# Last output tile's second token half in two quarters, each with its own statistics, transposes, scaling and store

## The chip, the cores and the metric

The kernel runs on one core of a Trainium2 chip. Its metric is the device time of one execution in microseconds (us), the median of several runs. A profile is one further execution, recorded by the hardware profiler. The engines of a core are TensorE (PE: matmuls, with weight loads as PEld), VectorE (DVE), ScalarE (ACT), GpSimd (POOL) and SyncE (SP, which here issues DMAs). Each has its own instruction queue and runs it in order; semaphores tie the queues together.

## The reference

One layer of a decoder on 512 tokens of width 2048, in float32. A conditioning vector gives six vectors of modulation (shift, scale and gate, twice). A first block mixes tokens in two ways and projects back; a second is an MLP with a hidden width of 8192 and a squared ReLU; a norm closes it:

```python
x = x + gate1 * merged
h = rmsnorm(x) * (1 + scale2) + shift2
x = x + gate2 * (relu(h @ w1) ** 2 @ w2)
out = x * rsqrt(mean(x * x, axis=-1) + 1e-6) * g_final
```

## The kernel before, in words

Activations are held transposed: a tile `x1[d]` of 128 x 512 has 128 of the 2048 features in its partitions and the 512 tokens in its columns, and there are sixteen. A float32 product is made of three matmuls in the fp32r type: weights and activations are split in a high and a low part (`wh`, `wl`; the activations carry both), and high-high, high-low and low-high are summed in PSUM (lines 174 to 176, and 894 to 896 for a part of the columns). The conditioning comes first, then the projections, attention and the gated merge with matmuls of 512 columns. Most of the MLP runs as "product units" (lines 1120 to 1123), whose matmuls have 256 columns. What they leave of the second weight matrix is a last pass over a part of the hidden width, tile by tile.

That pass ends in `fin_last`. Feature tiles 0 to 13 are finished before it. It takes tiles 14 and 15 in halves of 256 tokens. `tile` multiplies a half (twelve matmuls, from `hs` tiles as the moving operand), adds the product times the gate to `x1` (VectorE), squares the sum (ScalarE) and multiplies it by the final gain (VectorE). `post` works on a half's two rows of 128 tokens, numbered r = 0 to 3. `fin_stats` sums the squares over the features with matmuls of one column into a PSUM bank (`msf`): the sum of the earlier tiles in `sq_box["f"]`, then the squares of tile 14, then of tile 15. It takes the root on ScalarE and its reciprocal on VectorE, into a small tile `rf`. `to_rows` transposes the feature tiles with TensorE into PSUM (`nt`) and copies them (line 988 on VectorE, line 990 on ScalarE) into `nat` tiles, which have tokens in their partitions and 1024 features in their columns (z = 0 or 1). `fin_out` scales each `nat` tile by `rf` in two pieces of 512 columns, one on VectorE and one on ScalarE, and sends each piece to the output with a DMA that SyncE issues (line 1018).

In the product units the work stands on the engines in the order of the code (`manual_schedule`, lines 1275 to 1366). In the tail behind them a scheduler places instructions by their dependences when the program is built; the lines below give the pieces there, not their final order. Tiles live in pools in on-chip memory. `pw` holds the streamed weights (`wr`), the split weights (`wh`, `wl`, whose matrix in the product units begins 16 elements into the tile, `shift=16` at line 1160) and the small tiles (`small`), among them `rf`. The pools `sb` (most activation tiles, by `k4`: `h`, `mh`, `t`, `ya`, `yb`, `nat`, `sq`), `xw` and `win` (`hw`) lie behind it. `hs` is allocated from the other end.

Of the kernel before, what the change touches and what calls it, by code (L numbers as in the profile page):

```python
# [13 lines left out]
AF = mybir.ActivationFunctionType  # L14
# [4 lines left out]
D = 2048  # L19
# [8 lines left out]
SF = 8  # L28
# [16 lines left out]
def _body(tc, x, c, w_ada, b_ada, g_mix, w_in, b_in, g_v, b_v, w_s, b_s, w_oa, w_ob, w_out,  # L45
# [5 lines left out]
    pe, act, dve, pool = nc.tensor, nc.scalar, nc.vector, nc.gpsimd  # L51

    with tc.tile_pool(name="const", bufs=1) as cp, \
# [6 lines left out]
        def nm(s):  # L60
            cnt[0] += 1
            return f"{s}_{cnt[0]}"
# [17 lines left out]
        def k4(shape, s, dt=F32):  # L80
            return pools["sb"][1].tile(shape, dt, name=nm(s), tag="k4", bufs=k4_bufs[0])
# [13 lines left out]
        def bank(s):  # L95
            return pp.tile([128, T], F32, name=nm(s), tag="mm", bufs=6)

        def misc(s):
            return pp.tile([128, T], F32, name=nm(s), tag="ms", bufs=2)

        def small(shape, s, bufs=2):
            return pw.tile(shape, F32, name=nm(s), tag=f"sm{shape[1]}", bufs=bufs)
# [83 lines left out]
        epsc = cp.tile([128, 1], F32, name="epsc")  # L186
# [671 lines left out]
        x1 = {}  # L858
# [8 lines left out]
        sq_box = {}  # L867
# [22 lines left out]
        HALF = [slice(0, 256), slice(256, 512)]  # L890

        def mm3h(ps, wh, wl, a, start, stop, hs):
            kw = dict(skip_group_check=True)
            pe.matmul(ps, lhsT=wh, rhs=a[:, 0, hs], start=start, stop=False, **kw)
            pe.matmul(ps, lhsT=wh, rhs=a[:, 1, hs], start=False, stop=False, **kw)
            pe.matmul(ps, lhsT=wl, rhs=a[:, 0, hs], start=False, stop=stop, **kw)
# [66 lines left out]
        hid = {}  # L963
# [13 lines left out]
        def to_rows(d, rs):  # L977
            if d == 0:
                for r in range(NR):
                    for z in range(2):  # L980
                        nat[r, z] = k4([128, 1024], "nat")
            p = misc("nt")
            for r in rs:
                pe.transpose(p[:, r * 128:(r + 1) * 128], x1[d][:, r * 128:(r + 1) * 128], ident)
            for r in rs:
                o = nat[r, d // 8][:, (d % 8) * 128:(d % 8 + 1) * 128]
                if r % 2:
                    dve.tensor_copy(o, p[:, r * 128:(r + 1) * 128])
                else:
                    act.activation(o, p[:, r * 128:(r + 1) * 128], AF.Copy)  # L990

        wfin = {}

        def fin_stats(hf, sq):
            p = bank("msf")
            for z in range(3):
                for i in range(2):
                    r = hf * 2 + i
                    t = sq[z - 1][:, i * 128:(i + 1) * 128] if z else sq_box["f"][:, r * 128:(r + 1) * 128]
                    pe.matmul(p[:, i:i + 1], lhsT=t, rhs=ones[:, 0:1], start=z == 0 and i == 0, stop=z == 2,  # L1000
                              skip_group_check=True)
            rf = small([128, 2], "rf", 2)
            act.activation(rf, p[:, 0:2], AF.Sqrt, bias=epsc, scale=1.0 / D)
            dve.reciprocal(rf, rf)
            return rf

        def fin_out(hf, rf):
            ov = out.rearrange("(r i) d -> i r d", r=NR)
            for z in range(2):
                for i in range(2):  # L1010
                    r = hf * 2 + i
                    for q in range(2):
                        t = nat[r, z][:, q * 512:(q + 1) * 512]
                        if q:
                            act.activation(t, t, AF.Copy, scale=rf[:, i:i + 1])
                        else:
                            dve.tensor_scalar(t, t, rf[:, i:i + 1], None, op0=ALU.mult)
                        nc.sync.dma_start(out=ov[:, r, z * 1024 + q * 512:z * 1024 + (q + 1) * 512], in_=t)

        def fin_last():  # L1020
            act.activation(warm, x1[13][:, 0:1], AF.Sqrt, bias=epsc, scale=0.0)
            sq = []

            def tile(d, hf):
                p = bank("w")[:, 0:256]
                h, l = wfin[d]
                for k in range(SF // 2):
                    mm3h(p, h[:, k, :], l[:, k, :], hid["t"][:, k], k == 0, k == SF // 2 - 1, HALF[hf])
                t = x1[d][:, HALF[hf]]
                dve.scalar_tensor_tensor(t, p, mod(5, d), t, op0=ALU.mult, op1=ALU.add)  # L1030
                sq.append(k4([128, 256], "sq"))
                act.activation(sq[-1], t, AF.Square)
                dve.tensor_scalar(t, t, gfin_col[:, d:d + 1], None, op0=ALU.mult)

            def post(hf):
                rf = fin_stats(hf, sq[hf * 2:])
                for d in (14, 15):
                    to_rows(d, (hf * 2, hf * 2 + 1))
                fin_out(hf, rf)

            tile(14, 0)
            tile(15, 0)
            tile(14, 1)
            post(0)
            tile(15, 1)
            post(1)

        box4 = {}

# [323 lines left out]
        def t_epi(pr, j, p):  # L1373
            d = pr * 2 + j
            dve.scalar_tensor_tensor(x1[d], p, mod(5, d), x1[d], op0=ALU.mult, op1=ALU.add)
            add_square(x1[d], d, "f")
            dve.tensor_scalar(x1[d], x1[d], gfin_col[:, d:d + 1], None, op0=ALU.mult)

        for pr in range(7):
            ws_pair(pr * 256, list(range(SF // 2, SF)), w2_p, lambda k: hid["t"][:, k - SF // 2],  # L1380
                    lambda j, p, pr=pr: t_epi(pr, j, p))
# [4 lines left out]
        def w2_keep(d):  # L1386
            def bk(h, l):
                wfin[d] = h, l
                for e in (12, 13):
                    if d == 15:  # L1390
                        to_rows(e, range(NR))
                if d == 15:
                    fin_last()
            return bk
# [23 lines left out]
```

## Time and profile before

| | us |
|---|---|
| median of 3 runs | 2648.8 (2648.76 to 2649.16) |
| profiled execution | 2651.6 |
| its span, first to last instruction | 2649.9 |
| its time outside the span | 1.7 |
| TensorE busy in the span | 2564.9 (97%) |
| VectorE busy | 1836.0 (69%) |
| ScalarE busy | 1069.6 (40%) |
| mean granted TensorE clock | 0.986 of full speed |

The sums of busy time are averages over stages with different limits. The end of the program is read from the timeline of its last 16 us, from each engine's queue and from the chain of waits; the long stages from the number of matmuls in a stretch in which TensorE never idles, which gives the time from one start to the next (a matmul's own duration in the trace is longer, as matmuls overlap).

### The profile page before, as it was taken

What the parts mean: (1) busy time and instruction counts of PE and PEld (TensorE: products, weight loads), DVE (VectorE), ACT (ScalarE), POOL (GpSimd) and SP (SyncE); (2) the same over time, 40 slices, a digit from 0 to 9 for tenths busy, and PEclk for the clock granted to TensorE, in tenths of its full rate; (3) what the DMA queues carried; (4) which work ended last, traced back from release to release, by engine and by line L of the source; (5) the groups of instructions that cost most, each with busy time, mean ns of one, the idle gap of its engine ahead of it and who ended that gap; (6) DMA issues with size and microseconds to landing.
All of it is one profiled execution on the core that took longest, in us unless ns stands there. A gap on an engine that the chain in (4) does not pass through costs nothing.

```text
span 2649.9 us, 39933 instructions
## 1 busy us (share of the span) xinstructions
PE 2564.9 (97%) x16339; PEld 2329.3 (88%) x16339; DVE 1836.0 (69%) x2392; ACT 1069.6 (40%) x1533; POOL 231.5 (9%) x254
## 2 busy tenths in 40 slices
PE   5999999999999999999999999999988999999988
PEld 4889878888888888888888999999987999999986
DVE  6894563657454453555358898989874888888876
ACT  4322232342222222232365666666663333333334
POOL 4120210000000000001100011111110000000003
PEclk8999999999999999999999999999999999999999
DMA  9973574646364564656424566666678656565642
GB/s 322 305 237 100 159 176 119 188 132 214 94 216 140 174 199 129 219 186 207 150 68 161 192 205 213 202 216 201 217 250 330 223 195 223 195 223 195 223 163 80
DMA packets 403273, 506.15 MB, mean 191 GB/s; under 512 B 14414, under 2 KB 345842, under 8 KB 398482
## 3 DMA queue, kind: packets, MB, share of 16 engines
q1 hardware_dynamic: 384304, 439.40, 52.1%
q0 software_dynamic: 18624, 64.15, 6.3%
q8 instruction: 128, 2.10, 0.3%
q14 instruction: 55, 0.45, 0.1%
q10 hardware_dynamic: 162, 0.06, 0.0%
HBM read 435.36 MB, written 68.19 MB: 190 GB/s over the span
## 4 chain that ended last, share of the span: by engine, by line
PE 65%; issue 23%; DMA 5%; POOL 3%; DVE 2%; ACT 1%; SPq 0%; POOLq 0%; ACTq 0%; DVEq 0%
PE w L176 11%; PE w L174 11%; PE w L175 11%; PE x L1120 7%; PE x L1121 7%; PE x L1123 7%; POOL hid_d L1231 2%; PE v L453 1%; PE v L454 1%; PE v L455 1%; PE q L175 1%; PE q L176 1%; PE q L174 1%; PE va L730 1%; PE va L728 1%
## 5 line engine op out<-in xcount | busy, mean ns | idle before, releaser
L142 ACT ACTIVATE wh<-wr 128x1024 fp32r<-128x1024 f32 (+2 forms) x269 | 270.4, 1007 | 796.0 <-PE w L175 535.2
L143 DVE TENSOR_TENSOR wl<-wr,wh 128x1024 fp32r<-128x1024 f32 (+2 forms) x257 | 318.7, 1241 | 368.5 <-ACT wh L142 359.3
L1120 PE MATMUL x<-hw,wh 128*128 128x256 f32 x1568 | 367.9, 277 | 11.3 <-ACT wh L142 11.3
L1121 PE MATMUL x<-hw,wh 128*128 128x256 f32 x1568 | 367.7, 277 | 0.0
L174 PE MATMUL w<-h,wh 128*128 128x512 f32 x896 | 351.8, 393 | 0.8 <-ACT wh L142 0.8
L176 PE MATMUL w<-h,wl 128*128 128x512 f32 x896 | 349.6, 390 | 0.8 <-DVE wl L143 0.8
L175 PE MATMUL w<-h,wh 128*128 128x512 f32 x896 | 349.2, 390 | 0.0
L142 ACT ACTIVATE wh<-raw 128x896 fp32r<-128x896 f32 (+1 forms) x240 | 238.8, 1000 | 177.2 <-PE x L1121 117.4
L1120 PEld LDWEIGHTS x<-hw,wh 128*128 128x128 f32 x1568 | 295.3, 188 | 11.7 <-ACT wh L142 11.7
L1121 PEld LDWEIGHTS x<-hw,wh 128*128 128x128 f32 x1568 | 295.3, 188 | 0.0
L143 DVE TENSOR_TENSOR wl<-raw,wh 128x896 fp32r<-128x896 f32 (+1 forms) x240 | 275.8, 1149 | 9.8 <-ACT wh L142 9.8
L142 ACT ACTIVATE wh<-s 128x896 fp32r<-128x896 f32 (+1 forms) x180 | 176.9, 1000 | 161.6 <-PE x L1121 160.1
L143 DVE TENSOR_TENSOR wl<-s,wh 128x896 fp32r<-128x896 f32 (+1 forms) x180 | 207.0, 1150 | 38.5 <-ACT wh L142 38.5
L1123 PE MATMUL x<-hw,wl 128*128 128x256 f32 x1568 | 214.4, 276 | 0.0
L1120 PE MATMUL x<-h,wh 128*128 128x256 f32 x896 | 208.8, 276 | 0.5 <-ACT wh L142 0.5
L1121 PE MATMUL x<-h,wh 128*128 128x256 f32 x896 | 208.7, 276 | 0.0
L176 PEld LDWEIGHTS w<-h,wl 128*128 128x128 f32 x896 | 168.6, 188 | 36.6 <-DVE wl L143 1.3
L174 PEld LDWEIGHTS w<-h,wh 128*128 128x128 f32 x896 | 168.6, 188 | 35.6 <-ACT wh L142 1.3
L175 PEld LDWEIGHTS w<-h,wh 128*128 128x128 f32 x896 | 168.7, 188 | 34.4
L1123 PEld LDWEIGHTS x<-hw,wl 128*128 128x128 f32 x1568 | 194.8, 188 | 0.0
L273 DVE SCALAR_TENSOR_TENSOR acc<-xk,cact,acc 128x1024 f32<-128x1024 f32 x112 | 149.1, 1348 | 51.0 <-DMA xk<-in_w_ada_dram 49.6
L1120 PEld LDWEIGHTS x<-h,wh 128*128 128x128 f32 x896 | 168.2, 188 | 0.9 <-ACT wh L142 0.9
(282 smaller groups left out, 5115.1 us busy)
## 6 DMA issues: line engine op xcount, KB each, us to landing
wr<-in_w_in_dram SPq DMA_DIRECT2D x144, 512.0 KB, 4.0
xk<-in_w_ada_dram SPq DMA_DIRECT2D x128, 512.0 KB, 5.1
hw<-hid_d SPq DMA_DIRECT2D x34, 1792.0 KB, 7.4
raw<-in_w_dram SPq DMA_DIRECT2D x28, 2048.0 KB, 10.0
hid_d<-g POOLq DMA_DIRECT2D x84, 512.0 KB, 3.4
ld<-in_w_ada_dram SPq DMA_DIRECT2D x128, 256.0 KB, 5.8
wr<-in_w_out_dram SPq DMA_DIRECT2D x32, 512.0 KB, 3.8
wr<-in_w_dram SPq DMA_DIRECT2D x31, 512.0 KB, 3.8
```

Of the source, the lines that this page charges most:

```text
L142: act.activation(h, r, AF.Copy)
L143: (low or dve).tensor_tensor(l, r, h.bitcast(F32), op=ALU.subtract)
L174: pe.matmul(ps, lhsT=wh, rhs=a[:, 0, :], start=start, stop=False)
L175: pe.matmul(ps, lhsT=wh, rhs=a[:, 1, :], start=False, stop=False)
L176: pe.matmul(ps, lhsT=wl, rhs=a[:, 0, :], start=False, stop=stop)
L273: dve.scalar_tensor_tensor(a, w[:, q, :], s, a, op0=ALU.mult, op1=ALU.add)
L453: pe.matmul(vbox[r], lhsT=ah, rhs=wh[:, q, :], start=first, stop=False)
L454: pe.matmul(vbox[r], lhsT=ah, rhs=wl[:, q, :], start=False, stop=False)
L1120: pe.matmul(x, lhsT=h[:, i, :], rhs=a[:, 0], start=first and i == 0, stop=False, **kw)
L1121: pe.matmul(x, lhsT=h[:, i, :], rhs=a[:, 1], start=False, stop=False, **kw)
L1123: pe.matmul(x, lhsT=l[:, i, :], rhs=a[:, 0], start=False, stop=i == len(forms) - 1, **kw)
L1231: nc.gpsimd.dma_start(out=hid_d[n, :, k0:k1], in_=g.bitcast(F32))
```

## The change

`tile` takes any stretch of columns. Tile 15's second half becomes two calls of 128 columns, and `post` is called for r = 2 and for r = 3 apart, each with its own `msf` bank, root, reciprocal, transposes, scaling and stores. The first half stays. The small tiles `rf` get a third buffer, because three are alive where there were two; their tile is still 128 x 2, of which the quarters use one column.

```diff
--- before.py
+++ after.py
@@ -991,24 +991,23 @@
 
         wfin = {}
 
-        def fin_stats(hf, sq):
+        def fin_stats(rs, sq):
             p = bank("msf")
+            n = len(rs)
             for z in range(3):
-                for i in range(2):
-                    r = hf * 2 + i
-                    t = sq[z - 1][:, i * 128:(i + 1) * 128] if z else sq_box["f"][:, r * 128:(r + 1) * 128]
+                for i, r in enumerate(rs):
+                    t = sq[z - 1](r) if z else sq_box["f"][:, r * 128:(r + 1) * 128]
                     pe.matmul(p[:, i:i + 1], lhsT=t, rhs=ones[:, 0:1], start=z == 0 and i == 0, stop=z == 2,
                               skip_group_check=True)
-            rf = small([128, 2], "rf", 2)
-            act.activation(rf, p[:, 0:2], AF.Sqrt, bias=epsc, scale=1.0 / D)
+            rf = small([128, 2], "rf", 3)[:, 0:n]
+            act.activation(rf, p[:, 0:n], AF.Sqrt, bias=epsc, scale=1.0 / D)
             dve.reciprocal(rf, rf)
             return rf
 
-        def fin_out(hf, rf):
+        def fin_out(rs, rf):
             ov = out.rearrange("(r i) d -> i r d", r=NR)
             for z in range(2):
-                for i in range(2):
-                    r = hf * 2 + i
+                for i, r in enumerate(rs):
                     for q in range(2):
                         t = nat[r, z][:, q * 512:(q + 1) * 512]
                         if q:
@@ -1019,31 +1018,35 @@
 
         def fin_last():
             act.activation(warm, x1[13][:, 0:1], AF.Sqrt, bias=epsc, scale=0.0)
-            sq = []
-
-            def tile(d, hf):
-                p = bank("w")[:, 0:256]
+            sqs = {}
+
+            def tile(d, c0, c1):
+                p = bank("w")[:, 0:c1 - c0]
                 h, l = wfin[d]
                 for k in range(SF // 2):
-                    mm3h(p, h[:, k, :], l[:, k, :], hid["t"][:, k], k == 0, k == SF // 2 - 1, HALF[hf])
-                t = x1[d][:, HALF[hf]]
+                    mm3h(p, h[:, k, :], l[:, k, :], hid["t"][:, k], k == 0, k == SF // 2 - 1, slice(c0, c1))
+                t = x1[d][:, c0:c1]
                 dve.scalar_tensor_tensor(t, p, mod(5, d), t, op0=ALU.mult, op1=ALU.add)
-                sq.append(k4([128, 256], "sq"))
-                act.activation(sq[-1], t, AF.Square)
+                q = k4([128, c1 - c0], "sq")
+                act.activation(q, t, AF.Square)
+                for r in range(c0 // 128, c1 // 128):
+                    sqs[d, r] = q[:, r * 128 - c0:r * 128 - c0 + 128]
                 dve.tensor_scalar(t, t, gfin_col[:, d:d + 1], None, op0=ALU.mult)
 
-            def post(hf):
-                rf = fin_stats(hf, sq[hf * 2:])
+            def post(rs):
+                rf = fin_stats(rs, [lambda r, d=d: sqs[d, r] for d in (14, 15)])
                 for d in (14, 15):
-                    to_rows(d, (hf * 2, hf * 2 + 1))
-                fin_out(hf, rf)
-
-            tile(14, 0)
-            tile(15, 0)
-            tile(14, 1)
-            post(0)
-            tile(15, 1)
-            post(1)
+                    to_rows(d, rs)
+                fin_out(rs, rf)
+
+            tile(14, 0, 256)
+            tile(15, 0, 256)
+            tile(14, 256, 512)
+            post((0, 1))
+            tile(15, 256, 384)
+            post((2,))
+            tile(15, 384, 512)
+            post((3,))
 
         box4 = {}
```

The third buffer lengthens pool `pw`, and so everything in `sb`, `xw` and `win` begins 32 bytes further in each partition. In the program as built the first `sb` tile moves from byte 64,832 to 64,864 and `hw` from 95,552 to 95,584, that is from 64 past a multiple of 128 to 96 past one. The tiles `wh` and `wl`, `hs` and `qk` stay (64 past a multiple of 128; the shifted weights of the product units at a multiple of 128). Up to the last tile the order on every engine is the same as before, and GpSimd's is the same throughout.

On TensorE the program ended so before: the last three of twelve products of tile 15 (`w` is their PSUM tile, `hs` the hidden activations), then statistics and transposes of the half at once. "x2" after a row is two such instructions in a row.

```order
L894 MATMUL w_24269<-hs_23753,wh_24141 128x256
L895 MATMUL w_24269<-hs_23753,wh_24141 128x256
L896 MATMUL w_24269<-hs_23753,wl_24142 128x256
L1000 MATMUL msf_24286<-ones,sq_23774 128x1 x2
L1000 MATMUL msf_24286<-ones,sq_24230 128x1 x2
L984 MATMUL nt_24296<-ident,xp_17193 128x128 x2
L1000 MATMUL msf_24286<-ones,sq_24283 128x1 x2
L984 MATMUL nt_24301<-ident,xp_17193 128x128 x2
```

Now, from the statistics of r = 2 on, twelve products of the fourth quarter stand around them:

```order
L1000 MATMUL msf_24286<-ones,sq_23774 128x1
L1000 MATMUL msf_24286<-ones,sq_24230 128x1
L984 MATMUL nt_24293<-ident,xp_17193 128x128
L894 MATMUL w_24307<-hs_23753,wh_24141 128x128
L895 MATMUL w_24307<-hs_23753,wh_24141 128x128
L896 MATMUL w_24307<-hs_23753,wl_24142 128x128
L1000 MATMUL msf_24286<-ones,sq_24283 128x1
L894 MATMUL w_24307<-hs_23753,wh_24141 128x128
L895 MATMUL w_24307<-hs_23753,wh_24141 128x128
L984 MATMUL nt_24296<-ident,xp_17193 128x128
L896 MATMUL w_24307<-hs_23753,wl_24142 128x128
```

What moved: the statistics' last matmul for r = 2, on `sq_24283`, has three products of r = 3 ahead of it, and nine behind it.

On ScalarE the end was, from the last scaling of the first half on (`rf` the root, `nat` the rows, `nt` the transposes):

```order
L1015 ACTIVATE nat_23846<-nat_23846,rf_24240 128x512
L1032 ACTIVATE sq_24283<-xp_17193 128x256
L990 ACTIVATE nat_23848<-nt_24296 128x128
L1003 ACTIVATE rf_24293<-msf_24286,epsc 128x2
L1015 ACTIVATE nat_23847<-nat_23847,rf_24293 128x512
L990 ACTIVATE nat_23848<-nt_24301 128x128
L1015 ACTIVATE nat_23849<-nat_23849,rf_24293 128x512
L1015 ACTIVATE nat_23848<-nat_23848,rf_24293 128x512
L1015 ACTIVATE nat_23850<-nat_23850,rf_24293 128x512
```

It now is:

```order
L1014 ACTIVATE nat_23846<-nat_23846,rf_24240 128x512
L990 ACTIVATE nat_23848<-nt_24293 128x128
L1031 ACTIVATE sq_24283<-xp_17193 128x128
L1003 ACTIVATE rf_24290<-msf_24286,epsc 128x1
L1014 ACTIVATE nat_23847<-nat_23847,rf_24290 128x512
L990 ACTIVATE nat_23848<-nt_24296 128x128
L1014 ACTIVATE nat_23848<-nat_23848,rf_24290 128x512
L1031 ACTIVATE sq_24321<-xp_17193 128x128
L1003 ACTIVATE rf_24328<-msf_24324,epsc 128x1
L1014 ACTIVATE nat_23849<-nat_23849,rf_24328 128x512
L1014 ACTIVATE nat_23850<-nat_23850,rf_24328 128x512
```

What moved: a copy of r = 2's rows stands ahead of the square, both scalings of r = 2 come ahead of the square of r = 3, and a second root follows.

SyncE's last rows were, with the numbers of the `nat` tiles (3128 and 3129 are the two halves of r = 2's features, 3130 and 3131 those of r = 3; each row is two stores):

```order
L1018 DMA out_0_dram<-nat_3127_23846 128x512 x2
L1018 DMA out_0_dram<-nat_3128_23847 128x512 x2
L1018 DMA out_0_dram<-nat_3130_23849 128x512 x2
L1018 DMA out_0_dram<-nat_3129_23848 128x512 x2
L1018 DMA out_0_dram<-nat_3131_23850 128x512 x2
```

They are now:

```order
L1017 DMA out_0_dram<-nat_3127_23846 128x512 x2
L1017 DMA out_0_dram<-nat_3128_23847 128x512 x2
L1017 DMA out_0_dram<-nat_3129_23848 128x512 x2
L1017 DMA out_0_dram<-nat_3130_23849 128x512 x2
L1017 DMA out_0_dram<-nat_3131_23850 128x512 x2
```

What moved: r = 2's second half goes ahead of r = 3's first; number and size of the stores are the same.

## Rows read from the trace of the kernel before

**Rows 1.** The page's span and its 40 slices, TensorE's busy share in tenths

```profile
span 2649.9 us, 39933 instructions
...
PE   5999999999999999999999999999988999999988
```

**Rows 2.** Last two windows: length, busy us (instructions) by engine; clock, DMA share, GB/s

```profile
core 0: us, PE busy (x) PEld busy (x) DVE busy (x) ACT busy (x) POOL busy (x), PEclk, DMA share, GB/s
...
2634.00:2642.00 8.00, 3.20 (x27) 2.73 (x25) 5.26 (x16) 6.30 (x14) 0.00 (x0) 0.86 0.85 260
2642.00:2650.00 8.00, 0.00 (x0) 0.00 (x0) 0.00 (x0) 0.00 (x0) 0.00 (x0) 0.50 0.74 265
```

**Rows 3.** Timeline, SyncE's queue: start, us; all sixteen stores, then 9th, 13th, 16th

```profile
2634.71 10.51 SPq L1018 DMA_DIRECT2D out_dram<-nat  x16
...
2639.84 0.41 SPq L1018 DMA_DIRECT2D out_dram<-nat  x1
...
2642.51 0.68 SPq L1018 DMA_DIRECT2D out_dram<-nat  x1
...
2644.31 0.91 SPq L1018 DMA_DIRECT2D out_dram<-nat  x1
```

**Rows 4.** DMA, 2633 to 2650: 40 slices, issues (median to landing), line 1018's landing times

```profile
GB/s 0 0 0 0 0 19 328 381 361 333 241 227 222 284 390 386 400 400 275 255 337 400 289 304 362 405 352 376 415 405 386 415 352 270 178 135 10 0 0 0
...
out_dram<-nat SPq DMA_DIRECT2D x16, 256.0 KB, 4.4
...
DMA to landing us min/median/max: 2.9/4.4/4.9
```

**Rows 5.** Chain of waits, 2633 to 2650, its last piece: start, us, what

```profile
2640.45 0.61 ACTq L1414
```

**Rows 6.** Timeline of ScalarE and VectorE, 2634 to 2639

```profile
2634.28 2.56 ACT L1015 ACTIVATE nat<-nat,rf 128x512 f32<-128x512 f32 x4
2636.74 0.41 ACT L1032 ACTIVATE sq<-xp 128x256 f32<-128x256 f32 x1
...
2638.34 0.72 ACT L1015 ACTIVATE nat<-nat,rf 128x512 f32<-128x512 f32 x1 [0.23 <-DVE rf L1004]
...
2635.01 1.27 DVE L1017 TENSOR_SCALAR nat<-nat,rf 128x512 f32<-128x512 f32 x3
...
2638.14 0.17 DVE L1004 RECIPROCAL rf<-rf 128x2 f32<-128x2 f32 x1 [0.41 <-ACT rf L1003]
```

**Rows 7.** Timeline of TensorE, 2633 to 2638

```profile
2633.57 0.36 PE L894 MATMUL w<-hs,wh 128*128 128x256 f32 x1
...
2634.85 0.28 PE L895 MATMUL w<-hs,wh 128*128 128x256 f32 x1
...
2635.09 0.95 PE L1000 MATMUL msf<-ones,sq 128*128 128x1 f32 x8
2635.91 0.41 PE L984 MATMUL nt<-ident,xp 128*128 128x128 f32 x2
2637.20 0.60 PE L1000 MATMUL msf<-ones,sq 128*128 128x1 f32 x4 [0.88 <-ACT sq L1032]
```

**Rows 8.** Groups by line and shape: line, engine, count, busy us, mean ns

```profile
L1030 DVE SCALAR_TENSOR_TENSOR xp<-w,mods,xp 128x256 f32<-128x256 f32 x4 | 1.9, 481 | 0.0
...
L1375 DVE SCALAR_TENSOR_TENSOR xp<-w,mods,xp 128x512 f32<-128x512 f32 x1 | 0.8, 750 | 0.2 <-PE w L176 0.2
...
L174 PE MATMUL w<-hs,wh 128*128 128x512 f32 x120 | 49.0, 409 | 20.1 <-DMA hs<-hs_d 20.1
```

**Rows 9.** A window of the product units, columns of rows 2; two starts of 512 columns

```profile
1500.00:1600.00 100.00, 100.00 (x885) 100.00 (x884) 91.06 (x111) 67.67 (x106) 10.76 (x20) 1.00 0.62 207
...
1100.01 0.39 PE L174 MATMUL w<-ya,wh 128*128 128x512 f32 x1
...
1101.37 0.39 PE L174 MATMUL w<-ya,wh 128*128 128x512 f32 x1
```

**Rows 10.** The whole span, TensorE, line 1120 alone; then line 174 alone

```profile
0.00:2650.00 2650.00, 733.16 (x3136) 0.99 0.59 191
...
0.00:2650.00 2650.00, 639.37 (x1624) 0.99 0.59 191
```

## The prediction

> **What bounds the kernel now.** I read the page's slices first: TensorE is busy from one end of the span to the other but for the first slice [rows 1], so for most of the kernel a change matters if it alters what TensorE does. The exception is the end, where the edit stands, so next I split the last 16 us into two windows. From 2634 to 2642 TensorE is busy 3.2 us of 8, and from 2642 to 2650 no engine computes at all while the DMA engines are busy 0.74 of the time [rows 2]. The timeline of SyncE's queue says what is left: sixteen stores of the output, issued one behind the other from 2634.71 to 2645.22, with no wait shown between them [rows 3]. Each is 256 KB and needs 4.4 us (median) from issue to landing, 2.9 at the least [rows 4]. The chain of waits agrees from the other side: the last piece of work on it ends at 2641.06, nearly 9 us before the span does [rows 5]. So the end is set by issuing and moving sixteen stores, not by the arithmetic that makes them ready.
>
> **The change, part by part: the tail.** The first half of the tokens and its eight stores stay as they are. Of the second half:
>
> Products. Twelve matmuls of 256 columns, 0.12 us apart (2634.85 to 2635.09 is two of them), become 24 of 128 columns. No row shows this form at 128 columns. The nearest are the 256-column ones at 0.12 and the statistics' one-column matmuls: eight in the 0.82 us from 2635.09 until the next transposes start, about 0.11 each [rows 7], which bound it by the load of their 128 columns of weights. I take 0.11; half of 0.12, 0.06, is the low end and 0.22, two such loads, the high one. The first twelve, from 2633.57, then end near 2634.9 instead of 2635.09. That wins nothing: the addition of the products to x stands behind three scalings of the first half on VectorE, which run from 2635.01 to 2636.28 [rows 6].
>
> Third quarter (r = 2). The addition takes 0.48 us at 256 columns and 0.75 at 512 [rows 8], so some 0.35 at 128, from 2636.19. ScalarE is held by its four scalings until 2636.84 [rows 6]; a copy, to which I give 0.2, now stands ahead of the square, and the square, 0.41 before, shrinks to about 0.3. It ends near 2637.2, as the old one did. Two records of statistics instead of four (from 2637.20 in [rows 7]) then stand between it and the root, about 0.22 less at 0.11 each, so the root's reciprocal comes at 2637.9 instead of 2638.14 and scaling begins near 2638.1 instead of 2638.34 [rows 6]. ScalarE and VectorE each scale two pieces: ready at about 2638.6, 2638.8, 2639.0 and 2639.6. SyncE takes up its ninth store only at 2639.84 [rows 3], so all four lie in wait as the old ones did.
>
> Fourth quarter (r = 3). Of its twelve products nine are queued on TensorE behind statistics that wait for the square at 2637.2: 9 x 0.12 and two transposes give an end near 2638.8. Addition 2638.9 to 2639.25, square behind ScalarE's last r = 2 scaling 2639.5 to 2639.8, statistics 2640.2, root 2640.5, reciprocal and a copy 2640.85, then two scalings on each engine: ready at about 2641.3, 2641.4, 2641.7 and 2642.0, against 2641.06 for the last one now. The thirteenth store is issued at 2642.51 and the sixteenth at 2644.31 [rows 3]. So the added statistics lie wholly beside queued stores, with 1.2 us to spare at the tightest. With 0.22 us a product this quarter is 0.5 us later still, and is covered too. Beyond the 1.2 us lies a second cover: a store that lands 4.4 us after its issue where 2.9 is possible has some 1.5 us of queue in front of it [rows 4].
>
> Stores. The number, size and issuing engine are the same; stores 11 to 14 change places. From below: 16 x 0.256 MB at the best slice's 415 GB/s is 10.1 us, and they occupy about 12.8 us from 2635.5 to 2648.3 [rows 4], so 2.7 us is the most that a smoother stream could give. From above I allow 2 us, if the fourth quarter came at 2644.5 (twice the delay worked out, and more) and SyncE stood idle before it. I take 0, since nothing on the issuing side changes.
>
> **The part that is not in the tail.** The third buffer of the small tile moves every tile of the pools sb, xw and win by 32 bytes in each partition, from 64 to 96 past a multiple of 128. Those hold the moving operand of most matmuls. The count: each of L1120, L1121 and L1123 has 3136, of L174, L175 and L176 1504 (1624 less the 120 on hs, which doesn't move) [rows 8, 10]: 9408 of 256 columns and 4512 of 512. They run with TensorE 100% busy, so their pitch is the time: 885 in 100 us is 0.113 each, and six of 512 columns from 1100.01 to 1101.37 are 0.227 each [rows 9]. No row of this trace shows a moving operand at another place, so the price must be bounded. The nearest rows are the 0.12 of the tail, where the weights lie 64 past a multiple of 128, against 0.113 in the product units, where the kernel puts them at a multiple of 128 [rows 7, 9]. A start in another place can thus be worth 0.007 us a matmul, though for weights and for 64 bytes. At one such step each the whole costs 9408 x 0.007 + 4512 x 0.007 = 66 + 32 = 98 us; in the product units alone 66; at half a step there 33. From below the same steps with the other sign: VectorE is 91% busy beside them [rows 9], so a gain of up to 9% of that stage has room. I take 0, as the 512-column matmuls show no such step: their weights lie at 64 and their 0.227 is twice 0.113, not twice 0.12.
>
> The Trainium skill speaks to this in "SBUF — State Buffer", section "Specifications (TRN2)": it gives lines of 16 bytes, with full speed for repeated hits in one line. By that rule 32 bytes, two whole lines, change nothing and the sum stays as it is. But it would not foresee the 0.007 us of this trace for 64 bytes either, so it lowers the chance of the rivals below only a little.
>
> **Sum.** Profiled execution 2651.6 us, of which span 2649.9 and 1.7 outside. Tail 0 (-2.7 to +2), operands 0 (-66 to +98): 2651.6. The median of the runs is 2.8 lower at 2648.8, and that is my forecast.
>
> **The rivals.**
> 1. Slower: the moved operands cost TensorE time. Place: the product units, and perhaps the 512-column stages. Price 33, 66 or 98 us, so 2682, 2715 or 2747. It decides from 0.0006 us a matmul on (5.3 us over 9408). For it: TensorE has no idle time there to hide it, and the 0.113 against 0.12. Against it: that pair differs in the weights, and 512 columns show no step.
> 2. Faster: the same move takes a conflict away. 0.113 us for 256 columns at 2.4 GHz (256 / 2.4 = 107 ns) leaves 6 ns a matmul that something takes, and 0.227 leaves twice that. If the move took it away, the product units would give 0.006 x 9408 = 56 us, 2592; a third of it 19 us, 2630. For it: that remainder. Against it: it grows with the columns, so it looks like a rate and not like a start.
> 3. The tail moves after all: the fourth quarter's stores come late (2650.8 at +2), or the store stream runs smoother because r = 2 is wholly ready sooner (2646.1 at -2.7). Both are within what can't be told from no change: 0.2%, or 5.3 us, is about what a measurement of this kernel can tell.
> 4. The change doesn't bring the data sooner: r = 2 gains only 0.24 us in the working above, and its stores wait 0.2 to 2 us for SyncE anyway. That is part of the forecast.
>
> **How the numbers follow.** Forecast (no price for the move, tail near 0, 2646.1 to 2650.8): 0.50. Rival 3 at its ends, inside 0.2%: 0.04. Rival 1: 0.31, of which 0.11 near 2682 or below, 0.13 near 2715, 0.07 beyond. Rival 2: 0.15, of which 0.06 above 2630. So same 0.54, slower 0.31, faster 0.15. A range from 2630 to 2715 leaves out some 0.09 below and 0.07 to 0.1 above. The likeliest case's own range is 2646.1 to 2650.8.
>
> **What would show it.** Right: 885 or so matmuls per 100 us in the product units, and the tail's end as far behind the last product as now; sixteen stores issued back to back from about 2634.7 and no wait of SyncE before the thirteenth; last scaling near 2642.0 with the span ending near 2650. Rival 1 or 2: another count per 100 us in the same windows, for example 833 with 0.12 us, with the tail merely shifted. Rival 3: an idle stretch of SyncE between the twelfth store and the thirteenth. The forecast is wrong if the last product of w2 starts more than 5 us from where it does now, or if the stretch from it to the end changes by more than 2.7 us.

## The result and the profile after

The kernel after takes 2725.6 us (median of 4 runs, 2725.2 to 2726.7); the kernel before took 2649.0 beside it. The ratio is 1.0272 [1.0234, 1.0311]: 77 us slower, outside the range. On the chips of the experiments below the kernel before came out near 2647, near 2668 or, three times, at 2689 to 2695 us from run to run, so times there are read against these groups. The page of the profiled run gives the span and TensorE's slices:

```profile
span 2724.3 us, 39962 instructions
...
PE   5999999999999999999999999999988999999988
```

The span is 74.4 us longer than in [rows 1] and the slices look alike, so nothing stands out as a wait. The window of the product units answers to [rows 9], with the same columns:

```profile
1500.00:1600.00 100.00, 100.00 (x848) 100.00 (x847) 87.37 (x107) 64.50 (x101) 10.73 (x20) 1.00 0.60 199
```

848 matmuls in 100 us where there were 885: 0.1179 us each instead of 0.1130, at the full granted clock (1.00) and with TensorE busy throughout. (A window also counts the two or three matmuls that only overlap its edges. The mean from start to start, over the whole stage, is 118.3 ns against 113.3; the text uses these and calls this time the pitch.) The 512-column matmuls slowed too. In the timeline of the kernel after (start, duration) the second of these two starts six matmuls after the first:

```profile
1100.07 0.39 PE L174 MATMUL w<-h,wh 128*128 128x512 f32 x1
...
1101.47 0.39 PE L174 MATMUL w<-h,wh 128*128 128x512 f32 x1
```

That is 0.233 us each against 0.227. Where the time came in is read from the first and last starts of the product units, in the view of one source line (shortest, median and longest duration in ns, then first and last start). Before, line 1120:

```profile
L1120 PE MATMUL x<-hw,wh x1568: 276/276/580, 2035.4 to 2569.3; 128*128 128x256 f32 x196
...
L1120 PE MATMUL x<-h,wh x896: 276/276/384, 1434.1 to 1967.1; 128*128 128x256 f32 x180
```

After, where the same line is 1123:

```profile
L1123 PE MATMUL x<-hw,wh x1568: 277/281/582, 2086.2 to 2643.7; 128*128 128x256 f32 x196
...
L1123 PE MATMUL x<-h,wh x896: 277/282/385, 1461.3 to 2017.1; 128*128 128x256 f32 x180
```

All before the first product unit: +27.2 us (1434.1 to 1461.3). First product stage: 533.0 to 555.8, +22.8. Between the stages, where the moving operand is the unmoved `hs`: 68.3 to 69.1, +0.8. Second stage: 533.9 to 557.5, +23.6. From there to the first store's issue +0.2, and from it to the end of the span 15.2 to 15.0, -0.2. The sum is 74.4. So all of it lies in stages that the diff doesn't name, and the edited tail costs nothing.

The tail has one difference. SyncE's queue, answering to [rows 3]: all sixteen stores, then the twelfth and the thirteenth:

```profile
2709.35 10.48 SPq L1017 DMA_DIRECT2D out_dram<-nat  x16
...
2716.50 0.60 SPq L1017 DMA_DIRECT2D out_dram<-nat  x1
...
2717.49 0.33 SPq L1017 DMA_DIRECT2D out_dram<-nat  x1
```

The twelfth ends at 2717.10 and the thirteenth starts at 2717.49, so SyncE did wait for the fourth quarter, 0.39 us (the other stores follow one another within 0.10 us). The reason is on TensorE, answering to [rows 7]:

```profile
2711.89 0.58 PE L1000 MATMUL msf<-ones,sq 128*128 128x1 f32 x2 [1.28 <-ACT sq L1031]
2712.33 0.45 PE L894 MATMUL w<-hs,wh 128*128 128x128 f32 x1
2712.58 0.41 PE L895 MATMUL w<-hs,wh 128*128 128x128 f32 x1
```

and in the windows (length, TensorE busy, its granted clock, DMA share, GB/s):

```profile
2708.50:2710.50 2.00, 2.00 (x20) 1.00 0.16 55
2711.00:2712.30 1.30, 0.41 (x2) 0.74 1.09 317
2712.30:2714.50 2.20, 2.20 (x12) 0.50 1.05 304
```

The first quarter's products ran 0.11 us apart at 2.4 GHz. TensorE then waited 1.28 us for the square, and the nine products behind it ran at a granted 0.50, which is 1.2 GHz, 0.21 us apart: about 0.9 us more than planned. The stores already queued covered the wait of 0.39, as the 15.0 us to the end of the span show.

### The profile page after: what moved, and what is told of

The parts are those of the page before. It is cut to its first block, busy times and chain, and to the rows that moved or that the text cites. A ratio compares the mean times of both kernels' runs of the same rounds, so it can differ in the third digit from the quotient of the medians.

```text
span 2724.3 us, 39962 instructions
## 1 busy us (share of the span) xinstructions
PE 2645.9 (97%) x16351; PEld 2379.0 (87%) x16351; DVE 1850.1 (68%) x2395; ACT 1068.4 (39%) x1535; POOL 231.7 (9%) x254
## 4 chain that ended last, share of the span: by engine, by line
PE 69%; issue 23%; DMA 3%; POOL 2%; DVE 2%; ACT 1%; SPq 0%; POOLq 0%; ACTq 0%; DVEq 0%
PE w L174 11%; PE w L175 11%; PE w L176 11%; PE x L1123 7%; PE x L1124 7%; PE x L1126 7%; POOL hid_d L1234 2%; PE v L453 2%; PE v L454 2%; PE v L455 2%; PE q L175 1%; PE q L174 1%; PE q L176 1%; PE va L728 1%; PE va L730 1%
## 5 line engine op out<-in xcount | busy, mean ns | idle before, releaser
L1123 PE MATMUL x<-hw,wh 128*128 128x256 f32 x1568 | 382.4, 282 | 11.7 <-ACT wh L142 11.7
L1124 PE MATMUL x<-hw,wh 128*128 128x256 f32 x1568 | 382.2, 282 | 0.0
L174 PE MATMUL w<-h,wh 128*128 128x512 f32 x896 | 356.1, 397 | 0.0
L175 PE MATMUL w<-h,wh 128*128 128x512 f32 x896 | 354.0, 395 | 0.0
L1126 PE MATMUL x<-hw,wl 128*128 128x256 f32 x1568 | 222.4, 281 | 0.0
L1124 PE MATMUL x<-h,wh 128*128 128x256 f32 x896 | 217.4, 280 | 0.0
L1123 PE MATMUL x<-h,wh 128*128 128x256 f32 x896 | 216.9, 282 | 0.4 <-ACT wh L142 0.4
L1126 PEld LDWEIGHTS x<-hw,wl 128*128 128x128 f32 x1568 | 201.8, 189 | 0.0
```

The costliest lines, as they stand in the source:

```text
L174: pe.matmul(ps, lhsT=wh, rhs=a[:, 0, :], start=start, stop=False)
L175: pe.matmul(ps, lhsT=wh, rhs=a[:, 1, :], start=False, stop=False)
L1123: pe.matmul(x, lhsT=h[:, i, :], rhs=a[:, 0], start=first and i == 0, stop=False, **kw)
L1124: pe.matmul(x, lhsT=h[:, i, :], rhs=a[:, 1], start=False, stop=False, **kw)
L1126: pe.matmul(x, lhsT=l[:, i, :], rhs=a[:, 0], start=False, stop=i == len(forms) - 1, **kw)
```

## The experiments

Theory A: an operand that starts 32 bytes off a multiple of 64 costs TensorE a read, whichever operand it is. Theory B: the distance between the places of the moving operand and the weights decides. The rival to both: the split itself.

**One: the shift alone.**

```diff
-            rf = small([128, 2], "rf", 2)      # the kernel before
+            rf = small([128, 2], "rf", 3)
```

> The kernel before with a third buffer for rf and nothing else: the tiles of sb, xw and win stand 32 bytes further, the tail is the old one. If the 32 bytes are the cause: 2725 us, about +76 (the product units at 848 matmuls in 100 us, 512-column starts 0.234 apart, hs passes unchanged at 0.227). If the split of the tail has a part in it: 2649 for all of it, or something between 2649 and 2725.

Measured: 2726.2 us (4 runs, 2725.0 to 2726.8), ratio 1.0265 [1.0216, 1.0313]. Its windows (columns as above) in a stage of 512 columns and in the two product stages:

```profile
800.00:900.00 100.00, 100.00 (x434) 1.00 0.55 175
1500.00:1600.00 100.00, 100.00 (x848) 1.00 0.58 198
2250.00:2350.00 100.00, 100.00 (x847) 1.00 0.62 214
```

The old tail with the third buffer takes what the kernel after takes (2725.6), so it has the whole loss. The split has no part in it.

**Two: the split alone.**

```diff
-            rf = small([128, 2], "rf", 3)[:, 0:n]      # the kernel after
+            rf = small([128, 2], "rf", 10)[:, 0:n]
```

> The kernel after with ten buffers for rf, so that the tiles stand 256 bytes further than before instead of 32, at the same place in every 256. If the place decides: 885 matmuls in 100 us again, and the time is that of the split alone, 2648.8 us give or take 0.5 (in the two traces the stretch from the first store's issue to the end went from 15.1 to 14.9 us). If the split costs TensorE or the distance from the old place matters: 2725.

Measured: ratio 1.0019 [0.9985, 1.0054], lowest 2646.79 us against 2646.80 of the kernel before beside it. Both medians, 2667.5 and 2667.2, mix runs near 2647 and near 2668 us (experiment three shows a reason). The trace of it, of a run of 2646.8 us:

```profile
800.00:900.00 100.00, 100.00 (x447) 1.00 0.58 182
1500.00:1600.00 100.00, 100.00 (x885) 1.00 0.60 206
2250.00:2350.00 100.00, 100.00 (x885) 1.00 0.59 203
```

Both pitches are back. From the first store's issue (2630.20) to the end of the span (2645.1) it takes 14.9 us; no store waits, and the products behind the wait of TensorE (1.29 us here) happened to run 0.11 us apart. The split is worth nothing that can be measured.

**Three: the weights follow.** In the kernel after, `wh` and `wl` begin 32 bytes later in their tiles wherever they meet moved tiles:

```diff
-        def wsplit(r, shape, low=None, shift=0):
+        def wsplit(r, shape, low=None, shift=8):
...
-                    box["hl", u, j] = wsplit(s, [128, w, 128], shift=16)
+                    box["hl", u, j] = wsplit(s, [128, w, 128], shift=24)
```

(The passes over `hs` keep a shift of 0, which the lines of `ws_pair` and `w2_keep` hand on.)

> The kernel after with the split weights wh and wl also begun 32 bytes later in their tiles (product units 96 bytes in instead of 64, all others that meet moved tiles 32 in instead of 0). Theory A, that an operand's own start 32 past a multiple of 64 costs TensorE a read: nothing comes back, since now both operands start there; 2725 us or more, up to 2790. Theory B, that the distance of the moving operand from the weights decides: all distances are those of before; 113 and 227 ns again, 2649 us. In the trace of after the matmuls of 256 columns with both operands 96 past a multiple of 128 keep the 120 ns they had with both at 64, which speaks for B.

Measured: median 2650.5 us, ratio 0.9984 [0.9948, 1.0019]; ten runs from 2643.3 to 2670.6. Both operands of these matmuls now start 32 bytes off, and the time is that of before: theory A falls, B holds. Its trace is of a run of 2670.6 us and shows something new:

```profile
800.00:900.00 100.00, 100.00 (x447) 1.00 0.57 182
1500.00:1600.00 100.00, 100.00 (x852) 1.00 0.59 198
2250.00:2350.00 100.00, 100.00 (x884) 1.00 0.59 203
```

The second product stage ran at the old pitch (884 in 100 us, 113.3 ns), the first at 117.8 ns (852) from its beginning to its end, with the same program and the same places. 4704 matmuls at 4.5 ns are 21 us, the step between the two groups of times of experiment two. So at the good distance a stage can run at the slower pitch in some executions, here from its first matmul to its last; that the kernel before does the same in one stage at 2668 us, and in both near 2690, fits its times, but no trace here caught it.

**Four: 64 bytes.**

```diff
-            rf = small([128, 2], "rf", 2)      # the kernel before
+            rf = small([128, 2], "rf", 4)
```

> The kernel before with four buffers for rf: the tiles stand 64 bytes further, at a multiple of 128. Theory A: 64 is a whole step, so nothing is lost, 2649 us, or some gain. Theory B: in the product units the distance becomes a multiple of 128, as in the matmuls of the tail that take 120 ns, so 6.7 ns x 9408 = 63 us slower there; 512 columns now have the distance 64, for which no row stands: 2712 us if they keep 227 ns, 2742 if they go to 234.

Measured: 2724.2 us (4 runs, 2720.0 to 2726.3), ratio 1.0253 [1.0195, 1.0310].

```profile
1500.00:1600.00 100.00, 100.00 (x836) 1.00 0.58 195
```

120.0 ns in both product stages, as B foresaw for operands at one place: 9408 x 6.7 = 63 us. The 512-column matmuls came between B's two cases, 0.229 us apart (eight from 1100.15 to 1101.98), for some 10 us more. A whole step of 64 bytes is as bad as half of one, so "well aligned" is not the point.

**Five: the weights alone.** In the kernel before:

```diff
-                    box["hl", u, j] = wsplit(s, [128, w, 128], shift=16)
+                    box["hl", u, j] = wsplit(s, [128, w, 128], shift=24)
```

> The kernel before with the split weights of the product units 96 bytes into their tiles instead of 64; nothing else moves, no pool, no other matmul. Distance of the moving operand from the weights 32 past a multiple of 128, where before had 64 and after 96. Theory B (the distance decides, whoever is moved): 118 ns in both product stages, 9408 x 5 ns = 47 us, so 2696 us, and 227 ns kept at 512 columns. Theory A' (only the moved pools matter, through the moving operand's own start or through the engines and DMAs that read and write them): 113 ns and 2649 us.

Measured: 2696.2 us (2 runs, 2694.8 and 2697.5), 47 to 50 us above the lower group of the kernel before (2647.4). (The ratio, 1.0130 [1.0018, 1.0241], is to one run of that group and two near 2668 us; for this kernel and the six that follow such ratios lie between 1.0115 and 1.0166 and mix these groups, so the pitch of the trace is what counts.)

```profile
800.00:900.00 100.00, 100.00 (x446) 1.00 0.57 182
1500.00:1600.00 100.00, 100.00 (x845) 1.00 0.59 198
```

No pool moved, so no other engine's operand and no DMA's place did but those of `wh` and `wl` in their own tiles; the product units lose as in the kernel after (118.7 ns), and the 512-column stage keeps its count. With experiment three this shows the cause from both sides.

**Six to eleven: which distances.** Six gives `rf` six buffers (the pools 128 bytes further); the others are the kernel before with another `shift` in the line of experiment five: 20, 12, 32, 48 and 17.

> The kernel before with six buffers for rf: the pools stand 128 bytes further. If the distance counts by multiples of 128: as before, 113 and 227 ns, 2649 us (or one product stage at 118 ns, as the third experiment had, and then 22 us more). If it counts by 256: another pitch, 118 or 120 ns, and 2695 to 2712 us.

> The kernel before with the product units' weights 80 bytes into their tiles: distance 48 past a multiple of 128. If the price grows evenly from 113.3 ns at 64 to 118.3 at 32 and 96: 115.8 ns, 2672 us. If any distance but 64 is as bad as 32: 118.3, 2696 us. If what counts is that the two operands do not share a part of a line, 64 is not special and something between may be better: under 113 ns, under 2645 us.

> The kernel before with the product units' weights 48 bytes into their tiles: distance 80 past a multiple of 128, on the other side of 64. By the even price 115.8 ns and 2672 us, as at 48; by the rule that any other distance is bad 118.3 and 2696 us. A side that is better than the other would show that the order of the two reads counts, not only their distance.

> The kernel before with the product units' weights 128 bytes into their tiles: the moving operand stands 128 before them, modulo 256. If distances count by 128, as with both at one place: 120 ns in both stages, 9408 x 6.7 = 63 us, 2712 us. If they count by 256, it is a place of its own; a pitch of 113.3 or less in both stages in every run would be a better place than the one before has.

> The kernel before with the product units' weights 192 bytes into their tiles: distance 64 modulo 256, the distance of the sixth experiment with nothing else moved. If distances count by 256: 117.8 ns in both stages, 2690 us, and 227 ns at 512 columns. If they count by 128: as before, 113.3 ns, or 117.8 in one stage or both from run to run.

> The kernel before with the product units' weights 68 bytes into their tiles, 4 bytes more than before. If the start within a line of 64 bytes must be the same for both operands: 118 ns and 2694 us, as at 16 and 32 bytes. If a small step doesn't count (both still share the same 16 bytes' grid of starts only roughly): 113.3 ns, 2647 us.

In the table the distance is the weights' place less the moving operand's, modulo 256 bytes (the texts above count the other way, and by 128); the pitch is the mean from start to start in the product stages, both alike unless two are given:

| kernel | place moving, weights | distance | pitch, ns | us of its runs |
|---|---|---|---|---|
| before, two | 64, 128 | 64 | 113.3 | 2647 or 2668, before also 2689 to 2695 |
| three | 96, 160 | 64 | 117.8 and 113.3 | 2643 to 2671 |
| four | 128, 128 | 0 | 120.0 | 2720 to 2726 |
| after, one | 96, 128 | 32 | 118.3 | 2725 to 2727 |
| eight | 64, 112 | 48 | 117.8 | 2691, 2693 |
| eleven | 64, 132 | 68 | 118.3 | 2694, 2695 |
| seven | 64, 144 | 80 | 118.7 and 118.8 | 2698, 2703 |
| five | 64, 160 | 96 | 118.7 | 2695, 2697 |
| nine | 64, 192 | 128 | 118.7 | 2697, 2700 |
| ten | 64, 0 | 192 | 117.8 | 2688, 2691 |
| six | 192, 128 | 192 | 117.8 | 2696, 2716 |

Six and ten have one distance and one pitch, whichever operand was moved. Modulo 128 their distance is that of the kernel before. That it counts by 256, and not by 128 as I guessed in experiment four, is likely but not shown, because 117.8 ns is also the pitch that a stage at 64 fell into in experiment three. For 256 speaks that all four traced stages of six and ten have it, and by its time the other run of ten in both stages, where 23 runs of the kernel before have it, by their times, in 15 of 46. But six's other run, without a trace, is 20.0 us shorter than the traced one, which is the step of one product stage: at 192 too a stage may reach the good pitch. The same doubt holds for 48 (eight, 117.8 in two runs). The pitches of the other six distances, 118.3 to 120.0, stand in no trace at 64.

The even price of seven and eight fell (115.8 expected, 118.7 and 117.8 measured), and 4 bytes off the place of before cost as much as 32 (eleven, 118.3 as in the kernel after): of the nine distances tried in the product units only one gave 113.3 in a trace. Another stretch of the same traces bears the distance out. At lines 894 to 896 stand 96 matmuls of 256 columns that take `h` with weights at the start of their tiles, so that their distance is 0 before and 224 after. In the kernel before, the second of these rows starts 21 matmuls after the first:

```profile
1346.35 0.28 PE L894 MATMUL w<-h,wh 128*128 128x256 f32 x1
...
1348.87 0.28 PE L894 MATMUL w<-h,wh 128*128 128x256 f32 x1
```

In the kernel after, again 21:

```profile
1371.59 0.28 PE L894 MATMUL w<-h,wh 128*128 128x256 f32 x1
...
1374.04 0.28 PE L894 MATMUL w<-h,wh 128*128 128x256 f32 x1
```

That is 120.0 and 116.7 ns: the move that slowed the product units made these faster. In four (distance 192) they are 117.8 ns apart, as the product units of six and ten at that distance, and in six (128) 118.5.

At 512 columns the best of the four distances tried is 0 (0.227): 224 gave 0.233 in the kernel after, 192 gave 0.229 (four), and 128 gave 0.232 in six, where the second of these rows starts nine matmuls after the first:

```profile
1099.74 0.40 PE L174 MATMUL w<-h,wh 128*128 128x512 f32 x1
...
1101.83 0.39 PE L174 MATMUL w<-h,wh 128*128 128x512 f32 x1
```

That is where the rest of the time of six's traced run comes from. No place beat the old one, so there is no version to offer that beats the kernel before; the kernel after with its pools back at the old distance (two, or three) equals it.

## Why the prediction was wrong

**The tail** was right in its sum and not in all of its steps. The first twelve products at 0.11 us, the square's end beside the old one and r = 2's four pieces ahead of SyncE came as worked out. (The 10.1 us for the stores is 16 x 256 KiB, 4.2 MB, at 415 GB/s; with 0.256 MB each, as it is written, it would be 9.9.) The reciprocal of r = 2 did not come 0.24 us earlier: the two records of statistics took 0.58 us behind the wait, and it stands at 2712.80, which is 2638.16 on the clock of before, where [rows 6] has 2638.14. Nor did the fourth quarter come in time: I gave its nine queued products 9 x 0.12 us and counted 1.2 us to spare, but TensorE's wait of 1.28 us ahead of them, which stood in my own working as "statistics that wait for the square", was followed by a granted clock of 0.50. That it would fall could not be read from the rows of before, and the runs don't show what decides it. The clock stayed at 1.00 behind the wait of 0.88 us in the kernel before (first row), and in experiment two behind the same statistics and a wait of 1.29 us (second row; columns as in the windows of the tail above):

```profile
2637.20:2638.30 1.10, 0.88 (x6) 1.00 1.06 223
2632.70:2634.20 1.50, 1.46 (x14) 1.00 1.06 232
```

The spare time was gone and SyncE's wait of rival 3 came true with 0.39 us; the 1.5 us of stores queued in front took it, as the second cover of the prediction said. That the sum of the tail came out is owed to that cover, not to the steps of the fourth quarter.

**The step that failed** is "I take 0, as the 512-column matmuls show no such step: their weights lie at 64 and their 0.227 is twice 0.113". It looked for a price at one operand's own place. All rows of 512 columns had both operands at one place, and those of the product units had them 64 apart, so no row held the distance apart from the place; the 0.120 against 0.113 of [rows 7, 9], which I set aside as "for weights", was already the price of a distance (0 against 64). What the runs showed in place of the 0 is one mechanism, 5.0 ns on 9408 matmuls (47 us, where the prediction offered half a step, 33, or a whole one, 66) and 6.5 ns on 4512 (29 us, offered as 32), together 76 us by pitch and count; the trace has 46.4 in the product stages and 27.2 ahead of them. The count has a gap as well: in 960 more matmuls of 512 columns (lines 453 to 455 and 728 to 730) the moved tile is the weights, and they slowed too (line 729: 389 to 395 ns long in the mean). They are all ahead of the product units, so the 27.2 holds them, and not all of what the pitches add up to came through there. Rival 1 was right in place and sign; its 2715 and 2747 lie on either side of 2725.6, and the range ended at 2715 because the 512-column stages were put into the case beyond it.

**The Trainium skill's** "SBUF — State Buffer", "Specifications (TRN2)", gives lines of 16 bytes; by that the shift by two whole lines would cost nothing. The runs show 5 ns a matmul for it, and as much for 4 bytes; the measurement decides. The line is about accesses that hit one line, and not about moving operand and weights read beside each other (in [rows 9] matmuls and weight loads are both busy all of the 100 us), so it should not have lowered the chance of rival 1 even a little.

**What stays open.** Why one distance is good and why it differs for 256 and 512 columns: that the reads of the moving operand and the loads of the weights get in each other's way in the memory would fit the runs, but only the distances were shown. What makes a stage run at 117.8 ns at the good distance is open as well, and so are the modulus and whether 48 and 192 are bad in every run.

## What to carry to other kernels

A buffer added to a small tile moves every pool behind it. Before a change is read by its own instructions, list the tiles whose places it moves; where TensorE is busy throughout, compare the count of matmuls in 100 us before and after, and set the distance between moving operand and weights by hand (a pad in the pool, or an offset in the tile) so that it stays when buffers come and go.

Where a chain of small steps makes TensorE wait, as for 1.3 us here, what stands behind the wait should be worked out at both clocks: the same code ran on at 1.00 in two traces (two and three) and at 0.50 in one (the kernel after), with twice the time for each matmul.

## What the runs showed of the hardware

The pitch of fp32r matmuls of 256 columns, each with its own load of weights, changed with the distance between the places of the two operands: in the product units 113.3 ns at 64 bytes and 117.8 to 120.0 ns at the eight other distances tried, in a shorter stretch 120.0 at 0 and 116.7 at 224. A shift of 256 bytes changed nothing (two), and moving both operands by 32 bytes gave the pitch of before back (three). At 64 a stage of 4704 matmuls ran at either 113.3 or 117.8 ns, for the whole stage. Products of 128 columns ran 0.11 us apart at 2.4 GHz and 0.21 us at 1.2 GHz.
